# Strassen's seven block products in the last feed-forward stage of a float32 network, with grouped score products and one slot pool

## The chip, the cores and the metric

The kernel runs on one core of one Trainium2 chip, as one program. The metric is the device time of one execution in microseconds (us); lower is better. TensorE (PE) multiplies out of SBUF into PSUM, with its weight loads shown as a row of their own (PEld). VectorE (DVE), ScalarE (ACT) and GpSimd (POOL) do the elementwise work, and SyncE (SP) issues the loads of the weights.

## The reference

Two networks run one after the other on 512 tokens of width 1024, all in float32: two layers with retention, linear recurrence, dilated attention, memory cross-attention and a convolutional feed-forward block, then two layers whose normalised inputs are modulated by a conditioning vector. The last of all stages, ahead of the final norm, is the gated feed-forward block of the second of these layers:

```python
def modulate(h, shift, scale):
    return h * (1.0 + scale) + shift

def swiglu(h, w_gate, w_up, w_down):
    return (jax.nn.silu(h @ w_gate) * (h @ w_up)) @ w_down
```

Here h is 512 x 1024, w_gate and w_up are 1024 x 2816, w_down is 2816 x 1024, and the result is scaled by a gate per channel and added to x. In the layer's first half, a gated linear attention in two directions over four heads is computed; its scores are products of queries and keys that carry the decays.

## The kernel before, in words

Activations lie with channels on partitions: a tile is 128 channels x 512 tokens, so x is eight tiles. Every large product is split in three: an operand becomes a rounded part h and a remainder lo, both in the format that the page calls fp32r, and h*h, h*lo and lo*h are summed in PSUM. So a unit of weights (128 output channels by 1024 inputs) takes 8 x 3 matmuls of 512 columns each.

`raw` (L284) loads a unit by an SP DMA into one of 4 slots (`wr`). `unit` rounds it on ACT (L293, into `wh`, 3 slots) and takes the remainder on DVE (L294, into `wl`, 3 slots). `dx` (L1158) and `dxs` (L1169) issue the matmuls. A scheduler sets each engine's order from the order in the source and the data flow; each engine then runs its own list strictly in order, and semaphores make it wait for others.

`swiglu` is called twice; the second call (l = 1) has no context tokens (`c` is None). It modulates x into eight pairs of tiles (`modulate`, L1102 to L1110), the first 256 tokens ahead of the last 256. The first three weight units run on the first 256 tokens while the others are still being modulated (`dxs`, 144 matmuls of 256 columns). Then `gate_up` takes two units per hidden tile: Silu of the gate on ACT (L1515), the product with the up part on DVE (L1520), and `split` into h (L401, ACT) and lo (L402, DVE). The 22 hidden tiles come in three parts of 8, 8 and 6 (`PARTS`). After each part `gated` multiplies them by w_down, 8 output tiles, and adds into x (L1428). In the last part three of the eight output tiles are done by halves of the tokens, so that the statistics of the final norm start early.

In `cd_mixer`, the attention ahead of it, `head` computes for each of 4 heads and 2 directions four 128 x 128 blocks of scores in one PSUM bank. Each block sums a product over 128 rows (`ZK`, `ZQ`, L1786) and one over 64 rows (`Z2`, L1787), block after block, and a masked copy (L1788) takes the result. The projection of the mixer's output is done like the last part above: its last three output tiles finish in halves of the tokens, and the second halves (the jobs in `r["jobs"]`) are issued by `swiglu`, with steps of the modulation in between.

Tiles of 128 x 512 come from a pool of 66 slots; x tiles have a pool of 9, context tiles (256 wide) one of 9.

## Time and profile before

| what | us |
|---|---|
| median of 3 runs (lowest, highest) | 3156.91 (3155.29, 3159.71) |
| the profiled execution, own time | 3161.09 |
| its span, from first to last instruction | 3159.3 |
| PE busy in the span | 3102.5 (98%) |
| DVE, ACT, POOL busy in the span | 1779.6, 1118.1, 436.7 |

The profile is of one execution. Busy matmuls overlap each other, so PE's pace is read from how many start in a stretch, not from the duration of one. "x" ahead of a number counts instructions, "<-" ahead of an engine names what ended an idle stretch, and the granted clock is 1.00 at 2.4 GHz and 0.50 at 1.2 GHz.

### The profile page before, as it was taken

The numbers are of one execution on the slowest core, as the hardware profiler recorded it, in microseconds if no ns is written. First come the engines' busy times: TensorE is split into PE (matmuls) and PEld (weight loads), VectorE is DVE, ScalarE is ACT, GpSimd is POOL, SyncE is SP. The second block draws the span as 40 slices with busy tenths as digits, with TensorE's granted clock in tenths as the row PEclk, the third lists the DMA queues.
The fourth block names the chain that finished last, engine by engine and source line by source line (L and its number), as shares of the span: only waits on it lengthen the run. The fifth ranks groups of instructions, "written<-read, shape, count | busy, mean of one in ns | idle before, by whom it ended". The sixth has DMA issues, their size and how long they took to land. (4 is left out here: it accounts for less than half of the span.)

```text
span 3159.3 us, 40998 instructions
## 1 busy us (share of the span) xinstructions
PE 3102.5 (98%) x16292; PEld 2590.3 (82%) x16292; DVE 1779.6 (56%) x2894; ACT 1118.1 (35%) x1859; POOL 436.7 (14%) x375
## 2 busy tenths in 40 slices
PE   8999999999999999999999999999999999999998
PEld 6878888888877888888878778888888877788887
DVE  7767676575658857768654467342322453543333
ACT  2225353232445544423343545211212452342222
POOL 5023111010112111101121112000000310120001
PEclk9999999999999999999999999999999999999999
DMA  4224323333323423334342013232211220132222
GB/s 170 78 76 155 115 84 117 117 120 122 128 94 112 144 77 113 121 124 162 129 146 93 23 40 119 96 105 85 78 67 51 89 80 31 36 102 95 99 96 72
DMA packets 110355, 312.80 MB, mean 99 GB/s; under 512 B 12178, under 2 KB 17683, under 8 KB 110163
## 3 DMA queue, kind: packets, MB, share of 16 engines
q1 hardware_dynamic: 101968, 297.32, 27.7%
q10 hardware_dynamic: 8194, 12.86, 1.3%
q8 instruction: 128, 2.10, 0.3%
q14 instruction: 65, 0.52, 0.1%
HBM read 306.98 MB, written 3.15 MB: 98 GB/s over the span
## 5 line engine op out<-in xcount | busy, mean ns | idle before, releaser
L1158 PE MATMUL m<-t,wh 128*128 128x512 f32 (+1 forms) x4124 | 1093.0, 353 | 1.1 <-DVE t L1110 0.4
L293 ACT CAST wh<-wr 128x1024 fp32r<-128x1024 f32 (+2 forms) x485 | 487.8, 1008 | 1244.2 <-PE m L1158 422.2
L294 DVE TENSOR_TENSOR wl<-wr,wh 128x1024 fp32r<-128x1024 f32 (+2 forms) x485 | 579.2, 1195 | 450.1 <-ACT wh L293 438.3
L1158 PEld LDWEIGHTS m<-t,wh 128*128 128x128 f32 x4124 | 726.3, 190 | 115.3 <-issue 11.6
L312 PE MATMUL m<-t,wh 128*128 128x512 f32 (+1 forms) x2576 | 772.9, 383 | 0.0
L1158 PE MATMUL m<-t,wl 128*128 128x512 f32 (+1 forms) x2062 | 724.8, 352 | 0.5 <-DVE wl L294 0.5
L312 PEld LDWEIGHTS m<-t,wh 128*128 128x128 f32 x2576 | 474.1, 188 | 89.8 <-issue 1.0
L312 PE MATMUL m<-t,wl 128*128 128x512 f32 (+1 forms) x1288 | 491.5, 382 | 0.0
L1158 PEld LDWEIGHTS m<-t,wl 128*128 128x128 f32 x2062 | 390.8, 190 | 52.7 <-issue 1.9
L312 PEld LDWEIGHTS m<-t,wl 128*128 128x128 f32 x1288 | 242.7, 188 | 46.2 <-issue 0.7
L428 POOL TENSOR_TENSOR t<-t,t 128x512 f32<-128x512 f32 (+1 forms) x90 | 115.8, 1293 | 1162.8 <-ACT t L423 1162.4
L1062 DVE SCALAR_TENSOR_TENSOR t<-t,silc,t 128x512 f32<-128x512 f32 x280 | 219.0, 810 | 16.5 <-DMA t<-w_ada 15.8
L939 PE MATMUL m<-t,wh 128*128 128x512 f32 x704 | 217.3, 390 | 0.0
L342 PE MATMUL m<-t,wh 128*128 128x512 f32 x496 | 160.1, 402 | 7.3 <-ACT wh L293 7.3
L939 PEld LDWEIGHTS m<-t,wh 128*128 128x128 f32 x704 | 131.9, 188 | 27.2
L906 POOL TENSOR_TENSOR t<-t,t 128x512 f32<-128x512 f32 x44 | 64.5, 1465 | 549.8 <-ACT t L905 540.2
L401 ACT CAST t<-t 128x512 fp32r<-128x512 f32 x116 | 72.0, 621 | 189.0 <-DVE t L1520 104.0
L939 PE MATMUL m<-t,wl 128*128 128x512 f32 x352 | 137.1, 389 | 0.0
L1428 DVE SCALAR_TENSOR_TENSOR x<-m,modt,x 128x512 f32<-128x512 f32 (+1 forms) x70 | 49.3, 705 | 154.2 <-PE m L1158 154.1
L411 POOL TENSOR_TENSOR s<-s,nh 128x4 f32<-128x4 f32 (+2 forms) x67 | 72.1, 1078 | 439.3 <-DVE s L471 161.3
L357 PE MATMUL m<-wh,t 128*128 128x512 f32 x384 | 123.2, 397 | 0.0
L342 PEld LDWEIGHTS m<-t,wh 128*128 128x128 f32 x496 | 93.6, 192 | 26.7 <-ACT wh L293 8.0
(387 smaller groups left out, 3405.7 us busy)
## 6 DMA issues: line engine op xcount, KB each, us to landing
t<-w_ada SPq DMA_DIRECT2D x192, 256.0 KB, 4.0
wr<-w_fi SPq DMA_DIRECT2D x88, 512.0 KB, 3.3
wr<-w_gu SPq DMA_DIRECT2D x88, 512.0 KB, 3.3
wr<-w_fo SPq DMA_DIRECT2D x32, 512.0 KB, 3.4
wr<-w_dn SPq DMA_DIRECT2D x32, 512.0 KB, 3.2
wr<-w_ev SPq DMA_DIRECT2D x24, 512.0 KB, 3.3
wr<-w_xk SPq DMA_DIRECT2D x16, 512.0 KB, 3.4
wr<-w_xv SPq DMA_DIRECT2D x16, 512.0 KB, 3.4
```

What stands on the lines that cost most here:

```text
L293: nc.scalar.copy(h[:, 0:e], r[:, 0:e])
L294: nc.vector.tensor_sub(lo[:, 0:e], r[:, 0:e], h[:, 0:e])
L312: nc.tensor.matmul(ps[:, 0:n], A[:, s], B[:, 0:n], start=c == 0, stop=c == tot - 1)
L342: self.nc.tensor.matmul(ps, A[:, s], B, start=k == 0 and i == 0, stop=k == K - 1 and i == 2)
L357: nc.tensor.matmul(pss[tb], A[:, ts], B[:, s], start=(u == 0 and j == 0 and i == 0), stop=(u == nu - 1 and j == kper - 1 and i == 2))
L401: nc.scalar.copy(h[:, 0:n], src[:, 0:n])
L411: self.nc.gpsimd.tensor_tensor(r, v, self.nh[:, 0:w], ALU.pow)
L428: e.tensor_tensor(st[0][:, 0:n], st[0][:, 0:n], sq[:, 0:n], ALU.add)
L906: nc.gpsimd.tensor_tensor(y, y, rb, ALU.mult)
L939: nc.tensor.matmul(ps[:, 0:n], A[:, s], B[:, 0:n], start=c == 0, stop=c == tot - 1)
L1062: nc.vector.scalar_tensor_tensor(acc[i], r, s, acc[i], ALU.mult, ALU.add)
L1158: nc.tensor.matmul(ps[:, s], A[:, ws], B[:, s], start=j == 0 and i == 0, stop=j == last and i == 2)
```

## The change

**The last feed-forward stage.** For l = 1 a new function `swiglu_w` replaces the loops. It takes two units of weights as one 2 x 2 block matrix and the activations as another (two groups of input tiles by two halves of the tokens), and forms the 2 x 2 result with seven block products (Strassen's scheme in Winograd's form) where before there were eight. A pair is a gate unit with its up unit, or two output tiles of w_down over three inputs each side.

- `w_pair` loads both units (r0 and r1). Four sums of halves of them, s0, s1, s3 and s2, are made on POOL in this order (`start`, L1580 to L1583 of the new file; width 512 for a gate pair, 384 for a w_down pair). Each of the seven products (m1, m5, m6, m3, m2, m7, m4 in order of issue) rounds its own weight block by `operand` (ACT L325, DVE L326), which is 512 or 384 columns wide, and then runs 12 (w_down: 9) matmuls of 256 columns (L1594).
- Bank A sums m1, m6, m7 and m4 one after the other, bank C sums m5 and m3. Partial values are taken out in between: on ACT after m1, m5 and m6, on DVE after m3 (L1613), m2 (L1618) and m7 (L1622); for these the next product into the bank has to wait. m4 of a pair is issued after m1 and m5 of the next pair (`w_push`).
- The activations need seven variants too. `w_first` makes those for m1 and m2, `w_combos` the other five, with two subtractions on DVE and two on POOL, casts and remainders. This is done once for the four pairs of input tiles, and for 9 pairs of the first 18 hidden tiles. The last 4 hidden tiles go through `gated` as before.
- There are 22 gate pairs and 12 w_down pairs (three rounds of four), in the order 7 gate, 4 down, 6 gate, 4 down, 6 gate, 4 down, 3 gate, and then `gated` on the rest.
- `modulate_f` writes the modulated x in float32 for this, in place of `modulate`.

**Grouped score products.** In `head`, the eight 64-row products of both directions are issued first, then the eight 128-row products, in two banks.

**Pools.** x and context tiles (two to a slot) come from the one pool, now 78 slots. Raw units have 3 slots instead of 4. Rounded operands are tiles of 512 columns with h and lo side by side, 8 slots (four units); so `unit` now issues two casts and two subtractions for a unit of 1024 columns everywhere in the kernel.

```diff
-NSLOT = 66
+NSLOT = 78
...
+def fm_units_eo(w):
+    k, m = w.shape
+    t = np.concatenate([w, np.zeros((24 * 128 - k, m), w.dtype)], axis=0).reshape(4, 6, 128, m)
+    t = np.concatenate([t[:3, [0, 2, 4, 1, 3, 5]], t[3:]], axis=0)
+    return fm_units(t.reshape(24 * 128, m), 6)
...
-        self.xp = E(tc.tile_pool(name="xp", bufs=9))
-        self.cx = E(tc.tile_pool(name="cx", bufs=9))
         self.A = E(tc.tile_pool(name="A", bufs=NSLOT))
...
-        self.wr = E(tc.tile_pool(name="wr", bufs=4))
-        self.wh = E(tc.tile_pool(name="wh", bufs=3))
-        self.wl = E(tc.tile_pool(name="wl", bufs=3))
+        self.wr = E(tc.tile_pool(name="wr", bufs=3))
+        self.wk = E(tc.tile_pool(name="wk", bufs=8))
...
+    def operand(self, src):
+        nc, n = self.nc, src.shape[-1]
+        k = self.wk.tile([128, 1024], F32R, tag="k", name=f"wk{self.n}")
+        nc.scalar.copy(k[:, 0:n], src)
+        nc.vector.tensor_sub(k[:, 512:512 + n], src, k[:, 0:n])
+        return k
     def unit(self, ap):
...
-        nc.scalar.copy(h[:, 0:e], r[:, 0:e])
-        nc.vector.tensor_sub(lo[:, 0:e], r[:, 0:e], h[:, 0:e])
-        return h, lo
+        ks = [self.operand(r[:, c:min(c + 512, e)]) for c in range(0, e, 512)]
+        return Part(ks, 0), Part(ks, 512)
...
+    def w_combos(self, t0, t1, first=None):
+        P, Q = slice(0, 256), slice(256, 512)
+        out = first or self.w_first(t0, t1)
+        u, v = self.T(), self.T()
+        nc.vector.tensor_sub(u[:, P], t0[:, Q], t0[:, P])
+        nc.gpsimd.tensor_tensor(u[:, Q], t1[:, Q], t0[:, Q], ALU.subtract)
+        nc.vector.tensor_sub(v[:, P], t1[:, Q], u[:, P])
+        nc.gpsimd.tensor_tensor(v[:, Q], t1[:, P], v[:, P], ALU.subtract)
+        h, lo = self.T(F32R), self.T(F32R)
+        nc.scalar.copy(h[:, P], t1[:, Q])
+        nc.vector.tensor_sub(lo[:, P], t1[:, Q], h[:, P])
+        out["m3"] = (h[:, P], lo[:, P])
+        h, lo = self.split(u)
+        out["m5"], out["m7"] = (h[:, P], lo[:, P]), (h[:, Q], lo[:, Q])
+        h, lo = self.split(v)
+        out["m6"], out["m4"] = (h[:, P], lo[:, P]), (h[:, Q], lo[:, Q])
+        return out
+    def w_first(self, t0, t1):
+        for name, t in (("m1", t0), ("m2", t1)):
+            k = self.T(F32R)
+            nc.scalar.copy(k[:, 0:256], t[:, 0:256])
+            nc.vector.tensor_sub(k[:, 256:512], t[:, 0:256], k[:, 0:256])
+            out[name] = (k[:, 0:256], k[:, 256:512])
...
+    def w_pair(self, a0, a1, xs, done):
+        hw = 128 * len(xs)
+        def start():
+            r0, r1 = self.raw(a0), self.raw(a1)
+            s = [self.T() for _ in range(4)]
+            add = nc.gpsimd.tensor_tensor
+            L, R = slice(0, hw), slice(hw, 2 * hw)
+            add(s[0][:, L], r1[:, L], r1[:, R], ALU.add)
+            add(s[1][:, L], s[0][:, L], r0[:, L], ALU.subtract)
+            add(s[3][:, L], r0[:, R], s[1][:, L], ALU.subtract)
+            add(s[2][:, L], r0[:, L], r1[:, L], ALU.subtract)
+            st["w"] = {"m1": r0[:, L], "m2": r0[:, R], "m4": r1[:, R], "m5": s[0][:, L], "m6": s[1][:, L], "m3": s[3][:, L], "m7": s[2][:, L]}
+            st["A"], st["mu"] = self.PM(), self.T()
+        def mul(name, bank, first, last):
+            w = self.operand(st["w"][name])
+            ps, n = st[bank], len(xs)
+            for k in range(n):
+                s, t = slice(k * 128, k * 128 + 128), slice(512 + k * 128, 640 + k * 128)
+                xh, xl = xs[k][name]
+                for i, (A, B) in enumerate(((w[:, s], xh), (w[:, s], xl), (w[:, t], xh))):
+                    nc.tensor.matmul(ps[:, 0:256], A, B, start=first and k == 0 and i == 0, stop=k == n - 1 and i == 2, skip_group_check=not first)
+        def m1():
+            start()
+            mul("m1", "A", True, False)
+            nc.scalar.copy(st["mu"][:, 0:256], st["A"][:, 0:256])
...
+        def m7():
+            mul("m7", "A", False, False)
+            nc.vector.tensor_add(st["m5"][:, 256:512], st["A"][:, 0:256], st["m5"][:, 0:256])
+        def m4():
+            mul("m4", "A", False, True)
+            done(st["top"], st["A"][:, 0:256], st["m5"][:, 256:512])
+        return list(zip((0, 1, 3, 4, 5, 6, 9), (m1, m5, m6, m3, m2, m7, m4)))
...
+    def swiglu_w(self, l, r):
...
+        late = self.modulate_f(x, r["sx2"], l, 3, ts, 256, H[1])
+        next(late)
+        next(late)
+        xs = [self.w_first(ts[k], ts[k + 4]) for k in range(4)]
+        self.run(late)
+        for k in range(4):
+            self.w_combos(ts[k], ts[k + 4], xs[k])
...
+        def gate_up(j):
+            def done(gate, up0, up1):
+                nc.scalar.activation(gate, gate, AF.Silu)
+                y = self.T()
+                nc.vector.tensor_mul(y[:, 0:256], up0, gate[:, 0:256])
+                nc.vector.tensor_mul(y[:, 256:512], up1, gate[:, 256:512])
+                if j >= 18:
+                    tail.append(self.split(y))
+                    return
+                ys.append(y)
+                if len(ys) == 2:
+                    hid.append(self.w_combos(*ys))
+                    ys.clear()
+            self.w_push((wi[j], wi[22 + j], xs, done))
+        def down(p, m, hs):
+            def done(top, b0, b1):
+                nc.vector.scalar_tensor_tensor(x[m], top, self.M(l, 5, 0, m), x[m], ALU.mult, ALU.add)
+                for s, b in zip(H, (b0, b1)):
+                    nc.vector.scalar_tensor_tensor(x[m + 1][:, s], b, self.M(l, 5, 0, m + 1), x[m + 1][:, s], ALU.mult, ALU.add)
+            self.w_push((wd[m * 4 + p], wd[m * 4 + 4 + p], hs, done))
...
+        return self.gated(f"w_dn{l}", lambda m: 4 * m + 3, tail, [], x, None, l, 5, halves=3)
     def swiglu(self, l, r):
         nc = self.nc
         x, c = r["x"], r["c"]
+        if not c:
+            return self.swiglu_w(l, r)
...
-            for d, SC in ((0, SCf), (1, SCb)):
-                ZQ, ZK = Z[d]
-                ps = self.PA()
+            pss = [self.PA(), self.PA()]
+            for d in range(2):
                 for j in range(4):
                     s = slice(j * 128, j * 128 + 128)
-                    nc.tensor.matmul(ps[:, s], ZK[:, s], ZQ[:, s], start=True, stop=False)
-                    nc.tensor.matmul(ps[:, s], Z2[d][1][P, s], Z2[d][0][P, s], start=False, stop=True)
+                    nc.tensor.matmul(pss[d][:, s], Z2[d][1][P, s], Z2[d][0][P, s], start=j == 0, stop=False)
+            for d in range(2):
+                ZQ, ZK = Z[d]
+                for j in range(4):
+                    s = slice(j * 128, j * 128 + 128)
+                    nc.tensor.matmul(pss[d][:, s], ZK[:, s], ZQ[:, s], start=False, stop=j == 3)
```

How the scheduler's order stands, at three places. Line numbers of the changed program are those of the new file.

DVE in the last stage, before: in one round of `gate_up` (tile names: wl and wh parts of weights, wr raw weights, m a PSUM bank, t tiles).

```order
L294 TENSOR_TENSOR wl3786_24903<-wr3786_24900,wh3786_24902 128x1024
L402 TENSOR_TENSOR t3778_24828<-t3774_24793,t3777_24827 128x512
L294 TENSOR_TENSOR wl3789_24936<-wr3789_24933,wh3789_24935 128x1024
L1520 TENSOR_TENSOR t3781_24862<-m3783_24870,t3781_24862 128x512
L294 TENSOR_TENSOR wl3793_24972<-wr3793_24969,wh3793_24971 128x1024
```

DVE in the last stage now, one gate pair (raw units wr4969 and wr4970) and what is left of the pair ahead of it (wr4950). In order: the operand of m1, L1613 of the pair ahead, m5, L1618 of the pair ahead, m4 of the pair ahead, m6, L1622 of the pair ahead, then m3, m2 and m7.

```order
L326 TENSOR_TENSOR wk4977_26142<-wr4969_26128,wk4977_26142 128x512
L1613 TENSOR_TENSOR t4965_26093<-m4958_26025,t4956_26008 128x256
L326 TENSOR_TENSOR wk4980_26160<-t4971_26132,wk4980_26160 128x512
L1618 TENSOR_TENSOR t4965_26093<-a4966_26095,t4956_26008 128x256
L326 TENSOR_TENSOR wk4981_26176<-wr4950_25997,wk4981_26176 128x512
L326 TENSOR_TENSOR wk4993_26219<-t4972_26133,wk4993_26219 128x512
L1622 TENSOR_TENSOR t4959_26026<-m4955_26007,t4959_26026 128x256
L326 TENSOR_TENSOR wk4994_26235<-t4974_26135,wk4994_26235 128x512
L326 TENSOR_TENSOR wk4997_26253<-wr4969_26128,wk4997_26253 128x512
L326 TENSOR_TENSOR wk4998_26269<-t4973_26134,wk4998_26269 128x512
```

Where two subtractions of 1024 columns stood for 48 matmuls of 512 columns, seven of 512 columns now stand for 84 matmuls of 256, with evictions between them. On ACT the casts stand in the same order, and the Silu of the pair ahead (L1673) stands between the casts of m4 and m6:

```order
L325 CAST wk4980_26160<-t4971_26132 128x512
L325 CAST wk4981_26176<-wr4950_25997 128x512
L325 CAST wk4993_26219<-t4972_26133 128x512
L325 CAST wk4994_26235<-t4974_26135 128x512
L1673 ACTIVATE t4965_26093<-t4965_26093 128x512
```

In this pair it stands behind the casts of m6 and m3, in the pair ahead of it between those of m4 and m6; both orders occur.

SP in the same place, the loads of three pairs with the engines that each waits for. There are three slots, so the second load of a pair goes into the slot of the first unit of the pair ahead. That is free when m2's operand of that pair has been taken on DVE and its s2 made on POOL.

```order
L317 DMA wr4949_25995<-w_gu1 128x1024 [waits DMAHW3_49,DVE_49]
L317 DMA wr4950_25997<-w_gu1 128x1024 [waits DMAHW4_49,DVE_49,Pool_49]
L317 DMA wr4969_26128<-w_gu1 128x1024 [waits DMAHW5_49,DVE_49]
L317 DMA wr4970_26130<-w_gu1 128x1024 [waits DMAHW6_49,DVE_49,Pool_49]
L317 DMA wr4999_26285<-w_gu1 128x1024 [waits DMAHW7_49,DVE_49]
```

Before, a load waited only for the remainder (L294) of the unit four ahead of it, and POOL had nothing to do here. POOL now, for a pair and the start of the next, with the two subtractions of `w_combos` (L1529, L1531) between them:

```order
L1580 TENSOR_TENSOR t4971_26132<-wr4970_26130 128x512
L1581 TENSOR_TENSOR t4972_26133<-t4971_26132,wr4969_26128 128x512
L1582 TENSOR_TENSOR t4974_26135<-wr4969_26128,t4972_26133 128x512
L1583 TENSOR_TENSOR t4973_26134<-wr4969_26128,wr4970_26130 128x512
L1529 TENSOR_TENSOR t4985_26201<-t4982_26192,t4962_26059 128x256
L1531 TENSOR_TENSOR t4986_26202<-t4982_26192,t4986_26202 128x256
L1580 TENSOR_TENSOR t5001_26289<-wr5000_26287 128x512
```

POOL's first sum of a pair reads the second raw unit, and L1529 ahead of the next pair's first sum reads the hidden tile (t4982) of the pair ahead.

PE in `head` before, and now:

```order
L1786 MATMUL a3433_22430<-t3272_21367,t3273_21368 128x128
L1787 MATMUL a3433_22430<-t3276_21371,t3277_21372 128x128
L1786 MATMUL a3433_22430<-t3272_21367,t3273_21368 128x128
L1787 MATMUL a3433_22430<-t3276_21371,t3277_21372 128x128
L1786 MATMUL a3433_22430<-t3272_21367,t3273_21368 128x128
```

```order
L2014 MATMUL a4377_23145<-t4176_22046,t4177_22047 128x128 x4
L2014 MATMUL a4378_23146<-t4178_22048,t4179_22049 128x128 x4
L2019 MATMUL a4377_23145<-t4172_22042,t4173_22043 128x128 x4
L2019 MATMUL a4378_23146<-t4174_22044,t4175_22045 128x128 x4
```

The 64-row and the 128-row products alternated 16 times per head, and now stand in two runs of eight (L2014 and L2019).

## Rows read from the trace of the kernel before

**Rows 1.** The page, busy time of each engine over the span.
```profile
PE 3102.5 (98%) x16292; PEld 2590.3 (82%) x16292; DVE 1779.6 (56%) x2894; ACT 1118.1 (35%) x1859; POOL 436.7 (14%) x375
```
**Rows 2.** Busy time by stretch: last stage in full run, and the heads.
```profile
2804.50:3119.00 314.50, 314.48 (x1387) 260.56 (x1388) 112.17 (x120) 85.06 (x105) 0.00 (x0) 1.00 0.29 98
...
2640.00:2742.00 102.00, 101.68 (x588) 77.04 (x587) 46.37 (x101) 28.89 (x54) 9.23 (x12) 1.00 0.04 11
```
**Rows 3.** Instructions of L1169 and L1158 in the last stage: ns min/median/max, starts.
```profile
L1169 PE MATMUL m<-t,wh x96: 278/284/562, 2784.2 to 2802.6; 128*128 128x256 f32 x96
...
L1158 PE MATMUL m<-t,wl x522: 279/390/501, 2804.5 to 3148.2; 128*128 128x512 f32 x162, 128*128 128x256 f32 x12
```
**Rows 4.** Timeline of PE, half-width matmuls of the last output tiles (start, us, count).
```profile
3144.12 0.40 PE L1158 MATMUL m<-t,wh 128*128 128x256 f32 x2
...
3145.20 0.40 PE L1158 MATMUL m<-t,wh 128*128 128x256 f32 x2
```
**Rows 5.** Who waited for whom in the last stage: total us, times, longest.
```profile
PE m L1158 <- DVE wl L294: 0.5, 1, 0.5
```
**Rows 6.** Groups by shape, 2740 to 3160 and whole span: busy us, mean ns.
```profile
L294 DVE TENSOR_TENSOR wl<-wr,wh 128x1024 fp32r<-128x1024 f32 x60 | 73.6, 1227 | 84.0 <-ACT wh L293 79.8
L293 ACT CAST wh<-wr 128x1024 fp32r<-128x1024 f32 x60 | 63.2, 1053 | 224.0 <-PE m L1158 151.4 <-issue 64.0 <-PE m L1169 8.5
L401 ACT CAST t<-t 128x512 fp32r<-128x512 f32 x24 | 14.9, 621 | 3.8 <-POOL t L1813 3.5
L1103 ACT ACTIVATE t<-t,modt 128x256 fp32r<-128x256 f32 x10 | 4.9, 503 | 2.1 <-DVE t L1102 2.1
L1100 ACT CAST t<-t 128x256 fp32r<-128x256 f32 x6 | 2.4, 398 | 0.1
...
L1428 DVE SCALAR_TENSOR_TENSOR x<-m,modt,x 128x512 f32<-128x512 f32 x26 | 19.5, 751 | 70.8 <-PE m L1158 70.8
L1428 DVE SCALAR_TENSOR_TENSOR x<-m,modt,x 128x256 f32<-128x256 f32 x12 | 5.8, 483 | 9.2 <-PE m L1158 9.2
...
L1523 DVE TENSOR_TENSOR t<-m,t 128x256 f32<-128x256 f32 x22 | 9.3, 425 | 16.9 <-PE m L1158 16.9
L1376 POOL TENSOR_TENSOR t<-t,nam 128x256 f32<-128x256 f32 x24 | 16.9, 738 | 105.5 <-DMA t<-nab 70.3 <-PE m L1158 35.1
```
**Rows 7.** DMA issues of weights: KB each, median us to landing.
```profile
wr<-w_gu SPq DMA_DIRECT2D x88, 512.0 KB, 3.3
...
wr<-w_dn SPq DMA_DIRECT2D x16, 384.0 KB, 2.8
```
**Rows 8.** Timeline of DVE and of POOL, each with the other idle.
```profile
2811.90 0.68 DVE L402 TENSOR_TENSOR t<-t,t 128x512 fp32r<-128x512 f32 x1
...
1928.79 1.29 POOL L428 TENSOR_TENSOR t<-t,t 128x512 f32<-128x512 f32 x1 [1.74 <-ACT t L423]
```
**Rows 9.** Timeline of DVE and POOL in the same stretches, both at work.
```profile
12.26 9.50 DVE L405 SCALAR_TENSOR_TENSOR t<-xin,vec,t 128x512 fp32r<-128x512 f32 x6
...
13.31 1.61 POOL L515 TENSOR_TENSOR t<-t,t 128x512 f32<-128x512 f32 x1
14.88 1.49 POOL L513 TENSOR_TENSOR t<-xin 128x512 f32<-128x512 f32 x1
...
1912.52 1.33 DVE L294 TENSOR_TENSOR wl<-wr,wh 128x512 fp32r<-128x512 f32 x1
```
**Rows 10.** Timeline of PE in a head: start, us, count.
```profile
2645.14 0.61 PE L1774 MATMUL a<-t,t 64*128 64x128 f32 x4
2645.59 1.03 PE L1776 MATMUL a<-t 64*128 64x256 f32 x4
2646.54 0.49 PE L1786 MATMUL a<-t,t 128*128 128x128 f32 x2
...
2647.38 0.49 PE L1786 MATMUL a<-t,t 128*128 128x128 f32 x2
```
**Rows 11.** Opening of the last stage: busy time by stretch, and PE's timeline.
```profile
2778.00:2782.00 4.00, 0.60 (x3) 0.39 (x4) 3.37 (x5) 1.67 (x3) 3.40 (x3) 0.78 0.86 262
2782.00:2786.00 4.00, 2.96 (x14) 2.88 (x15) 2.40 (x8) 3.02 (x7) 2.51 (x3) 0.50 0.34 125
...
2785.20 0.42 PE L1169 MATMUL m<-t,wl 128*128 128x256 f32 x1
2785.41 0.42 PE L1169 MATMUL m<-t,wh 128*128 128x256 f32 x1
```

More of the change, by code (lines that the diff above doesn't have):

```diff
@@ L223, in layout, with __init__, __getitem__ @@
     return a
+class Part:
+    def __init__(self, tiles, base):
+        self.tiles, self.base = tiles, base
+    def __getitem__(self, key):
+        c = key[1]
+        o = self.base + c.start % 512
+        return self.tiles[c.start // 512][key[0], o:o + c.stop - c.start]
 class Net:
@@ L242, in __init__ @@
         self.side = None
+        self.half = None
         self.early = []
@@ L248, in T, with X, C @@
         return self.A.tile([128, 512], dt, tag="t", name=f"t{self.n}")
+    def X(self):
+        self.n += 1
+        return self.A.tile([128, 512], F32, tag="t", name=f"x{self.n}")
+    def C(self):
+        if self.half is None:
+            self.n += 1
+            t = self.A.tile([128, 512], F32, tag="t", name=f"c{self.n}")
+            self.half = t[:, 256:512]
+            return t[:, 0:256]
+        t, self.half = self.half, None
+        return t
     def S(self, w=16):
@@ L1446, in gated @@
             wt = self.wt(w, u(m), len(yx))
-            t = self.xp.tile([128, 512], F32, tag="x", name=f"x{self.n}") if m < 8 - halves else x[m]
+            t = self.X() if m < 8 - halves else x[m]
             r["x"].append(t)
@@ new lines, in w_first, with w_push @@
+    def w_first(self, t0, t1):
+        nc = self.nc
+        out = {}
+        for name, t in (("m1", t0), ("m2", t1)):
[3 more added lines that the diff above has]
+            out[name] = (k[:, 0:256], k[:, 256:512])
+        return out
+    def w_push(self, pair=None):
+        q = self.queue
+        if pair is not None:
+            ev = self.w_pair(*pair)
+            t = 7 * self.pushed
+            self.pushed += 1
+            q += [(t + at, self.pushed, f) for at, f in ev]
+            q.sort(key=lambda e: e[:2])
+            until = t + 7
+        else:
+            until = None
+        while q and (until is None or q[0][0] < until):
+            q.pop(0)[2]()
@@ new lines, in w_pair, with m5, m6, m3 @@
+    def w_pair(self, a0, a1, xs, done):
+        nc = self.nc
+        self.tick()
+        hw = 128 * len(xs)
+        st = {}
+        def start():
[21 more added lines that the diff above has]
+            nc.scalar.copy(st["mu"][:, 0:256], st["A"][:, 0:256])
+        def m5():
+            st["C"], st["m5"] = self.PM(), self.T()
+            mul("m5", "C", True, False)
+            nc.scalar.copy(st["m5"][:, 0:256], st["C"][:, 0:256])
+        def m6():
+            mul("m6", "A", False, False)
+            nc.scalar.copy(st["mu"][:, 256:512], st["A"][:, 0:256])
+        def m3():
+            mul("m3", "C", False, True)
+            st["top"] = self.T()
+            nc.vector.tensor_add(st["top"][:, 256:512], st["C"][:, 0:256], st["mu"][:, 256:512])
+        def m2():
+            st["B"] = self.PA()
+            mul("m2", "B", True, True)
+            nc.vector.tensor_add(st["top"][:, 0:256], st["B"][:, 0:256], st["mu"][:, 0:256])
+        def m7():
[5 more added lines that the diff above has]
+        return list(zip((0, 1, 3, 4, 5, 6, 9), (m1, m5, m6, m3, m2, m7, m4)))
@@ new lines, in modulate_f @@
+    def modulate_f(self, x, st, l, j, out, n, s):
+        nc = self.nc
+        rstd, _ = self.stat_end(st, n)
+        yield
+        pb = self.bcast(rstd, n)
+        rb = self.T()
+        nc.scalar.copy(rb[:, 0:n], pb[:, 0:n])
+        yield
+        for k in (0, 4, 1, 5, 2, 6, 3, 7):
+            t, sc, sh = out[k][:, s], self.M(l, j + 1, 0, k), self.M(l, j, 0, k)
+            if k in (5, 2, 7):
+                nc.gpsimd.tensor_tensor(t, x[k][:, s], rb[:, 0:n], ALU.mult)
+                nc.scalar.activation(t, t, AF.Identity, bias=sh, scale=sc)
+            else:
+                nc.vector.scalar_tensor_tensor(t, x[k][:, s], sc, pb[:, 0:n], ALU.mult, ALU.mult)
+                nc.scalar.activation(t, t, AF.Identity, bias=sh)
@@ new lines, in swiglu_w @@
+    def swiglu_w(self, l, r):
+        nc, a = self.nc, self.a
+        x = r["x"]
+        H = (slice(0, 256), slice(256, 512))
+        ts = [self.T() for _ in range(8)]
+        mx = self.modulate_f(x, r["sx"], l, 3, ts, 256, H[0])
+        for i, job in enumerate(r["jobs"]):
+            job()
+            if i in (1, 2):
+                next(mx, None)
+        self.run(mx)
+        late = self.modulate_f(x, r["sx2"], l, 3, ts, 256, H[1])
[5 more added lines that the diff above has]
+            self.w_combos(ts[k], ts[k + 4], xs[k])
+        self.queue, self.pushed = [], 0
+        ys, hid, tail = [], [], []
+        wi, wd = a[f"w_gu{l}"], a[f"w_dn{l}"]
+        def gate_up(j):
[18 more added lines that the diff above has]
+            self.w_push((wd[m * 4 + p], wd[m * 4 + 4 + p], hs, done))
+        j = 0
+        for p in range(3):
+            while j < 6 * p + 7:
+                gate_up(j)
+                j += 1
+            hs = hid[0:3]
+            del hid[0:3]
+            for m in (0, 2, 4, 6):
+                down(p, m, hs)
+        while j < 22:
+            gate_up(j)
+            j += 1
+        self.w_push()
+        return self.gated(f"w_dn{l}", lambda m: 4 * m + 3, tail, [], x, None, l, 5, halves=3)
@@ L1565, in small @@
         def small():
-            return self.cx.tile([128, 256], F32, tag="c", name=f"c{self.n}")
+            return self.C()
         def rope(ps, scale, eng=nc.gpsimd):
```

29 lines of the change are left out of this document (15 added, 14 removed).

## The prediction

> **What bounds the kernel now.** I read the page's first line, then the windows, then who waited for whom, then durations by shape. The page gives PE 98% of the span, the others far less [rows 1]. The windows show the same where the change works: in the last stage's full run PE is busy all of the time and starts 1387 matmuls in 314.5 us, .227 us each, with DVE at 36%, ACT at 27% and POOL at nothing; in the heads PE is busy 101.68 of 102 us [rows 2]. So PE's own issue bounds both places. PE waited .5 us in all for a remainder from DVE [rows 5]. The stage begins at 2784.2 and its last matmul starts at 3148.2, so with that matmul's own .1 it takes 364.1 us [rows 3].
>
> **Fewer matmuls.** 256-column matmuls start every .120 us (3145.20 less 3144.12 over nine) [rows 4]. The new stage has 22 gate pairs of 84 and 12 w_down pairs of 63, together 2604: 312.5 us. `gated` on the last four hidden tiles adds 60 of 512 columns (13.6) and 72 of 256 (8.6): 22.3. If PE stayed the bound, the stage would take 334.8, a gain of 29.3. Per pair PE needs 10.1 (gate) or 7.6 (w_down).
>
> **The new chain.** A load takes the slot of the first unit of the pair ahead, and may not start before m2's operand of that pair is on DVE and its s2 on POOL. From that release to the next, in a gate pair: the load lands after 3.3 us [rows 7]; s0, which reads that unit, takes 1.29 on POOL alone [rows 8]; the cast for m5 .62 [rows 6]; then DVE, strictly in order, does the subtractions for m5, m4, m6, m3 and m2, five of .68 alone [rows 8], and two evictions from PSUM of 256 columns at .42 [rows 6]. That is 3.3 + 1.29 + .62 + 3.4 + .84 = 9.5, and some .2 for handovers: 9.7, just under PE's 10.1. Nothing hides an addition here: while this chain is late, PE has only m4 of the pair ahead to do.
>
> While DVE does these five, POOL does s1, s3 and s2. Such meetings cost time: with both at work, six DVE operations on SBUF operands took 9.50 (1.58 each), POOL's took 1.61 and 1.49, and a DVE subtraction of exactly this kind 1.33 against .68 alone [rows 9]. So one DVE and one POOL operation take about 1.58 together, and a meeting costs DVE .65 to .9. I count two of the three in full (s1 partly runs while DVE still waits for m5's cast): +1.8, **11.6 per gate pair** with the handovers. Ends: 10.1 without any meeting (PE is then the bound again), 12.5 with all three.
>
> In pairs with `w_combos` (nine), DVE has between m2's subtraction and the next m5's: m7 and the next m1 (1.36), two products (.85), five operations of 256 columns (2.1), two of 512 (1.36) and two evictions (.85), 6.5 us, where load, sum and cast give it 5.2: +1.3. The second product waits for m4 of that pair on PE (.6), and one more meeting falls there, as POOL's L1529 and L1531 (.74 each [rows 6]) stand ahead of s0 and push it back: **14.2**; without meetings 12.0. I worked the 34 pairs through with each engine's order; these are its means.
>
> A w_down pair: load 2.8 [rows 7], and between the 512- and 256-column rows about 1.0 on POOL, .5 on ACT and .55 on DVE for 384 columns: 2.8 + 1.0 + .5 + 2.75 + .84 evictions and 1.23 for the adds into x (.75 and .48 [rows 6]) = 9.1; two meetings of .6 make 10.3, one of four rounds' pairs has fewer and is near 9: mean **10.0**, without meetings 9.25.
>
> Pairs: 13 x 11.6 + 9 x 14.2 + 12 x 10.0 = 398.6.
>
> The Trainium skill, "SBUF — State Buffer", section "Who interferes with whom", says that a DVE instruction with two SBUF inputs contends with a GpSimd instruction that reads SBUF, and calls the shared ports an exclusive lock. Rows 9 agree that they meet, but there each pays part: 1.58 for both, not the 1.97 of one behind the other. By its lock for a whole instruction two meetings would cost 2 x 1.29 = 2.6 a pair instead of 1.8, 27 us more in all.
>
> **The opening.** Before, 144 half-width matmuls [rows 3] run while the second half of the tokens is modulated. Now only m1 (1.4 us) can run; m5 needs `w_combos` of both halves, for all four pairs of tiles. On ACT that is 16 modulations at .50, 8 casts at .40 for `w_first`, 4 x (.40 + 2 x .62) for `w_combos`, and three operands at .62 [rows 6]: 8.0 + 3.2 + 6.6 + 1.9 = 19.7, begun near 2782 (ACT busy 3.02 of the 4 us from there [rows 11]); DVE has as much. So m5 can't run through before some 2804, where PE could have gone on from 2785.6: 18 us, of which the first two pairs give back about 4, as their weights are ready and they run at PE's pace. I take **14**, between 8 (the split before was also paced by these engines) and 18.
>
> Stage: 398.6 + 14 + 22.3 = 434.9, against 364.1: **+70.8**.
>
> **Grouped scores.** In a head now, two alternating blocks take .84 (2646.54 to 2647.38), so eight 6.7; four 64-row matmuls that follow each other start within .45 (2645.14 to 2645.59), .112 each [rows 10]. Grouped, 32 matmuls at .112 are 3.6 and two changes of shape .3: 3.9. That gains 2.7 a head in a place where PE is the bound, **−10.9** for four; ends 0 (the wait for the banks moves to DVE's masked copies) and −12.
>
> **The rest.** The first operand at the kernel's start is 512 wide: a cast of .62 for 1.05 and a subtraction of .68 for 1.23, **−1.0**, once. Elsewhere two casts of 512 cost ACT .19 more per unit and DVE .13 [rows 6]; both lie beside PE's work, 24 matmuls or 5.4 us per unit, with DVE at 56% [rows 1]. Were that cover gone, each unit would cost up to .19; PE's .5 us of waiting [rows 5] speaks against it. Slots: three raw and four rounded units are as deep as four and three, and the 78 common slots hold what 84 or less held in three pools: nothing.
>
> Sum: 70.8 − 10.9 − 1.0 = +58.9 on the profiled execution's 3161.1: 3220.0. That execution lies 4.2 above the median of the runs, so I predict **3216**.
>
> **Rivals.**
> 1. The other side, faster: the chain through the three slots stays shorter than PE's time in nearly every pair. It has .4 us of room in a plain gate pair without meetings [rows 8], has none with one meeting, and the loads may land sooner when two follow each other. Then 334.8 + 14 − 364.1 − 11.9 = −27, 3130. It decides at a mean pair: gain and loss balance at (364.1 + 11.9 − 36.3) / 34 = 10.0 us, where PE needs 9.2 and I forecast 11.7. Rows 9 speak against it. Chance .13.
> 2. The meetings are hidden: 13 x 10.1 + 9 x 12.0 + 12 x 9.25 = 350.3 instead of 398.6, so +10.6, 3167. For it: subtractions from POOL's pause (load) are untouched. Near it lies no change (a mean pair of 10.0). Chance .18.
> 3. Every meeting counts, or each lasts a whole instruction: +.9 x 34 = +31, 3246; both, 3 x 1.29 a pair, +70, 3286. Chance .12. The lock of the Trainium skill's page on SBUF is this case; rows 9 bear it out only in part, so it gets no more.
> 4. The clock: ahead of the stage PE is busy only .60 of 4 us, and the granted clock falls from .78 there to .50 (1.2 GHz) in the next 4, with 256-column matmuls .21 apart [rows 11]. The forecast leaves PE idle some 2.5 us a pair. If one pair in four runs at that level (gate 84 x .21 = 17.6), 8 x 6 = +48: 3265. PE's idle time is in pieces of 1 to 2 us, between busy stretches. Chance .05.
> 5. That the stage's products aren't fewer can be left out: the program's order has them.
>
> **Numbers.** Forecast case .52, rivals .13, .18, .12, .05. The range of 3165 to 3262 leaves out rival 1, rival 4 and the far end of rival 3, some .2. A measurement tells .2% (6.3 us) from no change: faster .14 (rival 1 and a little of 2), same .03 (the crossing between rivals 1 and 2), slower .83.
>
> **What would show it.** In the profile after: some 2.4 us of PE idle per pair, with the operands' subtractions (L326) as what ended it; loads of w_gu1 that start right after m2's subtraction or s2; subtractions of 512 columns in the stage at a mean near 1.0, against .68, and POOL's sums above 1.29; PE idle near 2786 to 2804; heads about 2.7 us shorter each; the same matmul pace of .12. It is wrong if PE is busy over 97% of the stage (rival 1), if the subtractions stay at .68 (rival 2), or if the granted clock in the stage falls under .9 (rival 4).

## The result and the profile after

| | before | changed |
|---|---|---|
| median of the runs, us (4 runs each) | 3158.31 | 3251.30 |
| lowest and highest, us | 3155.29, 3164.78 | 3249.94, 3252.32 |
| span of the profiled execution, us | 3159.3 | 3249.5 |

The changed kernel takes 1.0288 times as long (95% interval 1.0276 to 1.0300), 93 us more. I had forecast 59 more (3216), with a range of 3165 to 3262; the time lies in it and on the side I gave .83.

The page's first line, which answers to [rows 1]: DVE has 269 us more to do and POOL 185 more, while PE's busy time is the same, as waits have taken the place of matmuls.

```profile
PE 3103.6 (96%) x17318; PEld 2632.8 (81%) x17318; DVE 2049.1 (63%) x3658; ACT 1295.8 (40%) x2565; POOL 621.4 (19%) x537
```

The last stage by stretch, for [rows 2, 11] (busy time of PE, PEld, DVE, ACT, POOL, then granted clock, DMA share, GB/s): the opening, the 34 pairs with their end, and `gated` on the rest.

```profile
2793.00:2813.40 20.40, 3.72 (x12) 2.84 (x12) 19.26 (x34) 12.35 (x28) 11.52 (x13) 0.50 0.00 0
2813.40:3217.00 403.60, 349.14 (x2602) 330.11 (x2602) 323.70 (x493) 197.42 (x418) 203.62 (x153) 0.96 0.26 83
3217.00:3238.00 21.00, 20.67 (x125) 18.28 (x126) 7.81 (x14) 7.23 (x20) 8.56 (x12) 1.00 0.01 2
```

The stage begins at 2793.0, and its last matmuls start near 3238.5, so it takes 445.5 us where it took 364.1: +81.4 (forecast +70.8). In the opening PE did 12 matmuls in 20.4 us.

One turn of the chain, from the chain of waits between 2880 and 2915 (start, us, what). This is the order that the prediction gave: load, s0, cast, then subtractions on DVE with evictions among them.

```profile
2881.17 4.02 DMA wr<-w_gu
...
2885.33 1.29 POOL t L1580
2886.65 0.63 ACT wk L325
...
2888.47 0.41 DVE t L1618
2888.88 1.53 DVE wk L326 x2
...
2891.84 0.41 DVE t L1622
2892.25 1.24 DVE wk L326 x3
```

s0 (L1580) is made once per pair. Its row by line (ns min/median/max, first and last start) gives the pairs' pace: 3196.3 less 2811.0 over 33 pairs is 11.68 us.

```profile
L1580 POOL TENSOR_TENSOR t<-wr x34: 1010/1288/1741, 2811.0 to 3196.3; 128x512 f32<-128x512 f32 x22, 128x384 f32<-128x384 f32 x12
```

Groups by shape between 2820 and 3215 (busy us, mean ns | idle before, and what ended it):

```profile
L326 DVE TENSOR_TENSOR wk<-t,wk 128x512 fp32r<-128x512 f32 x84 | 81.9, 985 | 34.6 <-ACT wk L325 34.6
L326 DVE TENSOR_TENSOR wk<-wr,wk 128x512 fp32r<-128x512 f32 x71 | 67.9, 956 | 6.0 <-ACT wk L325 5.9
...
L1583 POOL TENSOR_TENSOR t<-wr,wr 128x512 f32<-128x512 f32 x21 | 35.9, 1707 | 0.0
L1582 POOL TENSOR_TENSOR t<-wr,t 128x512 f32<-128x512 f32 x21 | 34.0, 1619 | 1.6
...
L1580 POOL TENSOR_TENSOR t<-wr 128x512 f32<-128x512 f32 x21 | 29.1, 1385 | 87.6 <-DMA wr<-w_gu 76.4 <-DVE t L1618 5.8 <-DVE x L1688 5.3
```

A subtraction of 512 columns takes .97 on average where it takes .68 alone [rows 8], and POOL's sums 1.39 to 1.71 where 1.29. POOL's first sum of the gate pairs waits 76.4 us for loads: the load stands in the chain.

The heads, PE's timeline, for [rows 10]: two runs of 16, and 2666.47 to 2670.33 is 3.86 us, where eight alternating block pairs took 6.7.

```profile
2666.47 1.95 PE L2014 MATMUL a<-t,t 64*128 64x128 f32 x16
2668.34 2.05 PE L2019 MATMUL a<-t,t 128*128 128x128 f32 x16
2670.33 0.71 PE L2003 MATMUL a<-t,t 64*128 64x128 f32 x4
```

But the program is 20.0 us late when the heads begin (L2003 first starts at 2663.75; before, L1774 at 2643.73), where I had expected to be 1 us ahead.

### The profile page after: what moved, and what is told of

Read it like the earlier page. It is cut to its first block, busy times and chain, and to the rows that moved or that the text cites. A ratio compares the mean times of both kernels' runs of the same rounds, so it can differ in the third digit from the quotient of the medians.

```text
span 3249.5 us, 45317 instructions
## 1 busy us (share of the span) xinstructions
PE 3103.6 (96%) x17318; PEld 2632.8 (81%) x17318; DVE 2049.1 (63%) x3658; ACT 1295.8 (40%) x2565; POOL 621.4 (19%) x537
## 4 chain that ended last, share of the span: by engine, by line
PE 68%; DVE 9%; issue 4%; DMA 4%; ACT 3%; POOL 3%; SPq 0%; ACTq 0%; POOLq 0%; DVEq 0%
PE m L1196 25%; PE m L350 19%; PE m L977 6%; PE m L380 4%; DVE wk L326 4%; PE m L395 3%; DMA wr<-w_gu 1%; PE m L1240 1%; DMA t<-w_ada 1%; DMA wr<-w_dn 1%; ACT wk L325 1%; POOL t L1580 1%; PE m L1207 1%; PE a L433 1%; PE m L1594 1%
## 5 line engine op out<-in xcount | busy, mean ns | idle before, releaser
L326 DVE TENSOR_TENSOR wk<-wr,wk 128x512 fp32r<-128x512 f32 (+2 forms) x912 | 673.9, 745 | 431.5 <-ACT wk L325 428.9
L325 ACT CAST wk<-wr 128x512 fp32r<-128x512 f32 (+2 forms) x912 | 552.5, 609 | 921.9 <-PE m L350 259.7
L1196 PE MATMUL m<-t,wk 128*128 128x512 f32 (+1 forms) x4752 | 872.5, 343 | 4.9 <-ACT t L439 1.3
L350 PE MATMUL m<-t,wk 128*128 128x512 f32 (+1 forms) x3864 | 859.5, 381 | 0.0
L1196 PEld LDWEIGHTS m<-t,wk 128*128 128x128 f32 x4752 | 742.2, 191 | 118.0 <-issue 12.9
L350 PEld LDWEIGHTS m<-t,wk 128*128 128x128 f32 x3864 | 696.8, 188 | 135.8 <-issue 1.7
L1594 PE MATMUL m<-t,wk 128*128 128x256 f32 x2232 | 311.5, 296 | 71.5 <-ACT wk L325 22.7
L1594 PEld LDWEIGHTS m<-t,wk 128*128 128x128 f32 x2232 | 289.1, 200 | 90.9 <-ACT wk L325 38.7
L977 PE MATMUL m<-t,wk 128*128 128x512 f32 x1056 | 242.0, 390 | 1.1 <-ACT t L439 0.8
L977 PEld LDWEIGHTS m<-t,wk 128*128 128x128 f32 x1056 | 197.8, 188 | 42.7 <-ACT t L439 1.3
L380 PE MATMUL m<-t,wk 128*128 128x512 f32 x744 | 180.9, 396 | 16.9 <-ACT t L442 10.8
L380 PEld LDWEIGHTS m<-t,wk 128*128 128x128 f32 x744 | 138.3, 190 | 46.3 <-ACT t L442 10.8
L439 ACT CAST t<-t 128x512 fp32r<-128x512 f32 x124 | 76.5, 621 | 223.4 <-DVE t L1749 111.7
L326 DVE TENSOR_TENSOR wk<-t,wk 128x512 fp32r<-128x512 f32 (+1 forms) x136 | 116.8, 873 | 49.7 <-ACT wk L325 49.3
L395 PE MATMUL m<-wk,t 128*128 128x512 f32 x576 | 139.2, 397 | 0.0
L440 DVE TENSOR_TENSOR t<-t,t 128x512 fp32r<-128x512 f32 x124 | 104.0, 842 | 49.3 <-ACT t L439 44.3
L325 ACT CAST wk<-t 128x512 fp32r<-128x512 f32 (+1 forms) x136 | 78.5, 580 | 124.4 <-POOL t L1580 86.0
L395 PEld LDWEIGHTS m<-wk,t 128*128 128x128 f32 x576 | 107.4, 190 | 21.3
```

What stands on the lines that cost most here:

```text
L325: nc.scalar.copy(k[:, 0:n], src)
L326: nc.vector.tensor_sub(k[:, 512:512 + n], src, k[:, 0:n])
L350: nc.tensor.matmul(ps[:, 0:n], A[:, s], B[:, 0:n], start=c == 0, stop=c == tot - 1)
L380: self.nc.tensor.matmul(ps, A[:, s], B, start=k == 0 and i == 0, stop=k == K - 1 and i == 2)
L395: nc.tensor.matmul(pss[tb], A[:, ts], B[:, s], start=(u == 0 and j == 0 and i == 0), stop=(u == nu - 1 and j == kper - 1 and i == 2))
L439: nc.scalar.copy(h[:, 0:n], src[:, 0:n])
```

## The experiments

Each median was taken beside runs of the kernel before on the same chip, but not all experiments ran on one chip. So where a few us matter, the ratio to the kernel before is given, with its 95% interval.

**Grouped scores alone.** The kernel before with the new loops in `head`.

> The kernel before with the grouped score products alone. My theory (the alternation of 64-row and 128-row products cost PE .42 us per two of them and PE bounds the heads): 10.9 us less, about 3147, and 3.9 us per head from its first 64-row product to its last 128-row one, against 6.7. Rival: the gain is lost in waits for the two banks or for the masked copies that now come later; then within 3 us of 3158. Second rival: the 11 us between the heads and the last stage's begin in the changed kernel came from the pools; then again no change here.

3147.22, ratio .9965 (.9952 to .9979). The 11 us are there without any other part of the change. This kernel is faster than both, and only the one with the common pool (below) is level with it.

**Everything but the last stage.** The changed kernel without `swiglu_w`:

```diff
-        if not c:
-            return self.swiglu_w(l, r)
```

> The changed kernel with the old loops in the last stage (and the old layout of w_down there); grouped scores and the pools stay. In the changed kernel the program stands 20 us behind the one before when the heads begin, where I had 1 us of gain. Theory: the pools and the halved operands cost these 20 us, whatever the last stage does: 3158 + 20 - 11 = 3167. Rival: the scheduler moved work because of the new last stage, and the pools cost nothing: 3158 - 11 = 3147.

3164.13, ratio 1.0011 (1.0002 to 1.0020): the first theory. Pools and halved operands cost 17 us against grouped scores alone by the medians, 15 by the ratios, and the new last stage 87 (3251.3 − 3164.1).

**Four raw slots with the old last stage.**

```diff
-        self.wr = E(tc.tile_pool(name="wr", bufs=3))
-        self.wk = E(tc.tile_pool(name="wk", bufs=8))
+        self.wr = E(tc.tile_pool(name="wr", bufs=4))
+        self.wk = E(tc.tile_pool(name="wk", bufs=7))
```

> As the kernel without Strassen's products, with 4 raw slots as before in place of 3, paid for by one operand slot (7 for 8). If the third raw slot less is what costs the 20 us (loads that start later), most of it comes back: 3147 to 3152. If halved operands (more instructions on ACT and DVE) or the common pool cost it, it stays at 3165 to 3170.

3162.73, with the same ratio, 1.0011. The missing raw slot, in exchange for one operand slot more, is not what costs the 17 us there.

**Halved operands alone, the common pool alone, and both.** Each on top of grouped scores, in the kernel before: `operand` and `Part` with six slots; `X` and `C` with `NSLOT = 79`; and both.

> The kernel before with grouped scores and operands of 512 columns (two casts and two subtractions per unit, six slots, three units deep as before); raw slots, x and context pools as before. With grouped scores alone the time was 3147, with all pools of the change 3164, and a fourth raw slot gave nothing back. Theory: halved operands cost the 16 us: 3160 to 3166. Rival: the common slot pool does: 3145 to 3150. A part of both lies between.

3156.44, ratio .9985 (.9976 to .9994): 9 us of the 17 by the medians, 6 of the 15 by the ratios, less than the theory asked.

> The kernel before with grouped scores and x and context tiles in the common pool (79 slots, the same memory in all); operands and raw slots as before. Theory (the halved operands cost the 16 us): 3145 to 3150. Rival (the common pool, whose slots come free in another order, does): 3160 to 3166.

3148.36, ratio .9955 (.9941 to .9969): the common pool costs nothing that can be measured.

> The kernel before with grouped scores, operands of 512 columns (six slots) and the common pool (79 slots), 4 raw slots. Alone, the operands took the 3147 of grouped scores to 3156 and the pool to 3148; all of the change but the last stage stands at 3164. Theory (the two costs add up, and what is left comes from the counts of slots, 78, 8 and 3): 3156 to 3159. Rival (together they cost more than apart): 3162 to 3166.

3157.92, ratio .9993 (.9984 to 1.0002), where the theory had it: 9 us by the ratios, which fits a sum of the two. The intervals leave each of these differences open by some 4 to 5 us, so the sum is not shown closely. The 5 to 6 us between this and 3163 or 3164 go with the numbers of slots (79 and 6 here, 78 and 7 or 8 there). Which of them, and how, stays open.

The profiles show where the time goes, though not why. If the kernel without `swiglu_w` and grouped scores alone are laid beside each other matmul by matmul, the first is 5.9 us behind at 1766 us and 18.4 at 2009. In that stretch PE's products of queries and keys (L1364, L1326 before) wait for the exponentials of a softmax on ACT (L1271, L1233 before). First grouped scores alone, then without `swiglu_w` (us, times, longest):

```profile
PE a L1326 <- ACT t L1233: 3.6, 4, 1.3
...
PE a L1364 <- ACT t L1271: 7.5, 5, 2.6
```

In the same stretch halved operands alone lose 6.3 us, and the common pool alone 7.8, which it had gained earlier.

**Four raw slots in the changed kernel**, the edit shown above.

> The changed kernel with 4 raw slots for 3 (and 7 operand slots for 8). A pair's second load then waits for m4's operand of two pairs before, and no longer for m2's and s2 of the pair ahead. Theory (load, sum, cast and five subtractions follow each other through the slot): the 3.4 us of the load leave the chain; the next bound is DVE, busy 82% from 2800 to 3140, so the 34 pairs fall from 403 us to 330 to 350, the whole to 3180 to 3200. Rival (DVE with its meetings is the bound already, and the slot only shows where it waits): under 15 us less, 3236 or more.

3182.95: 68 us less than the changed kernel, inside the theory's span. The pace falls to (3129.2 − 2804.2) / 33 = 9.85 us. Windows from 2830 to 3130, first of this kernel:

```profile
2830.00:3130.00 300.00, 285.41 (x2303) 278.28 (x2302) 296.23 (x442) 170.21 (x367) 189.25 (x139) 1.00 0.29 97
```

DVE is now busy 296 of 300 us: it is the bound, and no longer the load.

**One sum in place of four.** s1, s3 and s2 are left out, and m6, m3 and m7 read s0.

```diff
-            s = [self.T() for _ in range(4)]
+            s = [self.T()] * 4
...
-            add(s[1][:, L], s[0][:, L], r0[:, L], ALU.subtract)
-            add(s[3][:, L], r0[:, R], s[1][:, L], ALU.subtract)
-            add(s[2][:, L], r0[:, L], r1[:, L], ALU.subtract)
```

> The changed kernel with s0 alone made on POOL; s1, s3 and s2 are left out and m6, m3 and m7 take s0 in their place, so these products are not those of the reference. Theory (subtractions on DVE that meet POOL's sums take .98 us for .68, and that lies on the chain): plain gate pairs fall from 11.7 to 10.1 (PE), pairs with combinations from 14 to 12, w_down pairs from 10.3 to 9.3: some 50 us less, 3200. Rival (the meetings fall beside waits for the load): under 15 us less.

3191.94: 59 us less. In its groups by shape the subtractions, unchanged in number and size, are back at the duration that they have alone (window 2820 to 3130):

```profile
L326 DVE TENSOR_TENSOR wk<-t,wk 128x512 fp32r<-128x512 f32 x76 | 51.0, 682 | 28.2 <-ACT wk L325 28.2
L326 DVE TENSOR_TENSOR wk<-wr,wk 128x512 fp32r<-128x512 f32 x57 | 39.0, 684 | 16.3 <-ACT wk L325 16.3
```

This also takes away the time in which ACT's casts wait for s1, s3 and s2, so not all of the 59 is the meetings. The next run keeps the sums.

**The four sums on DVE.**

```diff
-            add = nc.gpsimd.tensor_tensor
+            add = nc.vector.tensor_tensor
```

> The changed kernel with the four sums of a pair on DVE in place of POOL. DVE gets 4 x .68 = 2.7 us more of work per gate pair, and no sum of a pair meets it. Theory (each meeting costs DVE .65 to .9, and s0 on DVE is .6 shorter): chain of 3.3 + .68 + .62 + 3.4 + .84 + 2.0 = 10.9 per plain gate pair for 11.7, so 15 to 30 us less, 3220 to 3236. Rival (meetings cost little, DVE's work counts): 2.0 to 2.7 us more per pair, 3300 or more.

3210.12: 41 us less, more than the theory gave, though DVE issues 136 operations more. It isn't the meetings alone, as s0 on DVE is also .6 shorter and stands in the chain. The pace is (3158.2 − 2811.2) / 33 = 10.52. Subtractions and sums all take their own time now:

```profile
L326 DVE TENSOR_TENSOR wk<-t,wk 128x512 fp32r<-128x512 f32 x72 | 49.4, 699 | 0.1
...
L1581 DVE TENSOR_TENSOR t<-t,wr 128x512 f32<-128x512 f32 x18 | 12.4, 690 | 0.5
```

Work of .68 per sum on the busier engine is cheaper than the same work beside it.

**Four raw slots, and the sums on DVE.** Both edits.

> The changed kernel with 4 raw slots and the four sums of a pair on DVE. With 4 slots alone DVE was busy 98% of the stage. Theory (then DVE's occupancy is the bound, and a sum on DVE costs it .68 where a sum on POOL costs it up to .9, but not every one on POOL meets a DVE operation): about the time of 4 slots alone, 3175 to 3205, with plain gate pairs at PE's 10.1 and pairs with combinations at 12 to 13. Rival (only meetings hold DVE): 3165 or less.

3173.34: 10 us less than four slots alone, just below the theory's span and above the rival's. So in this stage a sum on POOL costs more, on average, than the .68 that it takes on DVE. The pace is (3121.8 − 2804.0) / 33 = 9.63, near PE's own 9.2. Windows of this kernel, its opening and its pairs:

```profile
2784.60:2805.30 20.70, 3.72 (x12) 2.84 (x12) 19.64 (x35) 12.36 (x29) 9.28 (x11) 0.50 0.00 0
2830.00:3130.00 300.00, 295.60 (x2369) 287.00 (x2368) 289.61 (x578) 173.12 (x378) 21.82 (x18) 1.00 0.31 99
```

PE is busy 295.6 of 300 us, nearly as before the change. Still the kernel (ratio 1.0038) is 9 to 11 us slower than the one with the same slots and the old last stage (3162.73, ratio 1.0011): the opening of 20.7 us eats most of what the fewer products save.

**Two pairs ahead in the opening.** The first two gate pairs stand ahead of the second half's modulation, all seven products on the operands of m1 and m2; so the first two hidden tiles differ from the reference's.

```diff
-            self.w_push((wi[j], wi[22 + j], xs, done))
+            self.w_push((wi[j], wi[22 + j], first if j < 2 else xs, done))
...
+        gate_up(0)
+        gate_up(1)
+        self.run(late)
+        for k in range(4):
+            self.w_combos(ts[k], ts[k + 4], xs[k])
```

> The changed kernel with the first two gate pairs issued ahead of the modulation of the second 256 tokens, all seven products on the operands of m1 and m2; so the first two hidden tiles are not those of the reference, all work stays. Theory (PE idles 18 to 20 us in the opening because m5 waits for the combinations of all eight tiles, and two pairs are 20 us of PE's work): 10 to 18 us less, 3233 to 3241. Rival (ACT and DVE are full with modulation and combinations there, and the pairs' own operands stand in their queues): under 5 us less.

3245.88: 5.4 us less, nearly the rival's case (ratio 1.0267 against 1.0288). PE's timeline shows the wait moved behind the two pairs:

```profile
2817.96 3.04 PE L1594 MATMUL m<-t,wk 128*128 128x256 f32 x24
2831.83 1.10 PE L1594 MATMUL m<-t,wk 128*128 128x256 f32 x3 [10.83 <-ACT wk L325]
```

The work for the combinations has to be done all the same, and the two pairs' operands stood in its way on DVE. The edit also brought POOL's sums of the first pair forward, beside DVE's eight remainders of `w_first` (L1549): these took 8.36 us in a row where they took 4.07. So the place of the matmuls is not what holds the opening. That DVE does is argued from its 19.26 busy us of 20.4; no run takes work off it there.

## Why the prediction was right, and where it was too small

The time is 35 us above the 3216 that I gave. In the profiles, 10.6 of these lie in the last stage. Another 20.7 lie ahead of it: it begins 8.8 us later than before, where I had it 11.9 earlier. The last 4.2 are what I took off because the execution profiled before lay above its median; the changed kernel's does not.

**The chain and its pace: right in the mean, with luck.** I forecast 398.6 us for 34 pairs, 11.72 each; measured 11.68. The chain of waits shows load, s0, cast and subtractions in this order. But the parts were off and cancelled. From one s0 to the next, the twelve gate turns without `w_combos` took 12.4 us on average (forecast 11.6), the nine with it 12.5 (14.2), and the w_down turns 10.3 (10.0). The first is near the 12.5 that I had given for three meetings, where I counted two. The 2.6 us that I added for `w_combos` hardly show, as the load then lands beside DVE's work for it:

```profile
2949.85 1.28 POOL L1580 TENSOR_TENSOR t<-wr 128x512 f32<-128x512 f32 x1 [5.68 <-DMA wr<-w_gu]
...
2961.83 0.79 POOL L1531 TENSOR_TENSOR t<-t,t 128x256 f32<-128x256 f32 x1 [2.37 <-DVE t L1530]
2962.58 1.74 POOL L1580 TENSOR_TENSOR t<-wr 128x512 f32<-128x512 f32 x1
...
2974.82 1.29 POOL L1580 TENSOR_TENSOR t<-wr 128x512 f32<-128x512 f32 x1 [5.42 <-DMA wr<-w_gu]
```

The turn with `w_combos` (from 2949.85) takes 12.73, and its successor's s0 waits for no load; the turn without (from 2962.58) takes 12.24, and the next s0 waits 5.42 for its load.

Four slots gave 68 us, the sums on DVE 41, and both together 78, so the gains overlap. Four slots alone left 25 of the 93 us, the sums on DVE alone 52. Only with both was PE nearly the bound again.

**The meetings: right in size, wrong in kind.** The mean of .97 less .68, over seven subtractions, is 2.0 us per gate pair, where I counted 1.8 on the path. But I had read [rows 9] as each engine paying a part of a meeting, and that reading failed. Here is a turn on both engines, first POOL, then DVE:

```profile
2951.21 1.30 POOL L1581 TENSOR_TENSOR t<-t,wr 128x512 f32<-128x512 f32 x1
2952.59 1.62 POOL L1582 TENSOR_TENSOR t<-wr,t 128x512 f32<-128x512 f32 x1
2954.16 1.73 POOL L1583 TENSOR_TENSOR t<-wr,wr 128x512 f32<-128x512 f32 x1
...
2951.82 1.24 DVE L326 TENSOR_TENSOR wk<-t,wk 128x512 fp32r<-128x512 f32 x1 [1.91 <-ACT wk L325]
2952.98 1.77 DVE L326 TENSOR_TENSOR wk<-wr,wk 128x512 fp32r<-128x512 f32 x1
2954.68 0.41 DVE L1622 TENSOR_TENSOR t<-m,t 128x256 f32<-128x256 f32 x1
```

The first subtraction ends at 2953.06, .55 us after POOL's L1581 (2952.51). The second ends at 2954.75, .54 after L1582 (2954.21). The trace has this for every one of the 59 subtractions of 512 columns between 2820 and 3215 that began while POOL was at an operation: each ends .55 after that operation, whether it had .54 or 1.23 us left, and they take 1.44 on average. The 91 that met none took .68, and the four that began ahead of POOL's operation .69. With four raw slots it is the same, 68 of 68.

So the subtraction that comes second waits until POOL's whole operation is over, and a meeting costs what is left of it, .76 on average. POOL waits likewise: its 51 sums of 512 columns that began during such a subtraction (L326 or L440) took 1.66 on average for 1.29, and ended 1.14 after it. That is the exclusive lock that I had quoted from the Trainium skill, "SBUF — State Buffer", section "Who interferes with whom", and the trace agrees with it. My 1.29 per meeting for that case was too much, since the wait is only for what is left. L294 of [rows 9] shows it already. POOL's sum beside it began at 1912.00, so with the 1.29 of [rows 8] it ended near 1913.29, and L294 ended at 1913.85.

Rival 2 (meetings hidden) falls, as its sign, subtractions at .68, did not come and taking the sums away gave 59 us. How much of these 59, or of the 41, is meetings alone was not separated. Rival 1 falls with the pace.

**The opening: too small.** I took 14, from 18 less 4 that the first two pairs would give back. From the stage's begin to the first s0 it is 18.0, m5 went on 20.4 us after m1, and nothing came back: the second s0 stands 11.43 after the first (2811.01 and 2822.44). The step that failed is "the first two pairs give back about 4, as their weights are ready". With three slots the second pair's second load waits for m2's operand of the first pair like any other. With four slots, where it doesn't, the second s0 came 6.7 us after the first (2804.17 and 2810.88). The 18 itself was summed for ACT, which was busy only 12.35 us there; it was DVE, which I had put at "as much", that was. Also, the last part of those 20 us is a relay: for each pair of tiles DVE, POOL, DVE, POOL, ACT and DVE take turns, 3.4 us a round:

```profile
2805.87 0.41 DVE L1528 TENSOR_TENSOR t<-t 128x256 f32<-128x256 f32 x1
2806.31 0.42 DVE L1530 TENSOR_TENSOR t<-t,t 128x256 f32<-128x256 f32 x1
2806.66 0.42 DVE L1534 TENSOR_TENSOR t<-t,t 128x256 fp32r<-128x256 f32 x1
2807.02 2.31 DVE L440 TENSOR_TENSOR t<-t,t 128x512 fp32r<-128x512 f32 x2
2809.26 0.41 DVE L1528 TENSOR_TENSOR t<-t 128x256 f32<-128x256 f32 x1
```

**The end of the pairs: forgotten.** I gave each pair one pace. From the last s0 (3196.3) to the long run of `gated` (3217.3) it is 21.0 us, 9.3 more than a pace. The chain of waits there holds three loads of units of w_down, which come one after the other through the raw slots, and the split of a last hidden tile (L439), which stands on ACT behind the cast that waits for the third load:

```profile
3204.47 2.50 DMA wr<-w_dn
...
3208.42 2.48 DMA wr<-w_dn
...
3212.37 3.66 DMA wr<-w_dn
...
3216.75 0.53 ACT t L439
```

With four slots and the sums on DVE the same stretch is 14.6 us (3121.8 to 3136.4), 5.0 more than its pace. Opening +4 and this +9.3, less 1.6 on the pace and about 1 on `gated`, are the 10.6 by which the stage was under-sized.

**Grouped scores: right.** 10.9 forecast; 3.86 us per head as worked out, and 12 us between the medians of the two kernels, 11 by the ratio.

**"The rest": wrong, and the largest miss.** I put the halved operands and the pools at −1.0 because their work lies beside PE's. They cost 15 to 17 us: 6 to 9 the operands, nothing measurable the pool, 5 to 6 tied to numbers of slots and open. The sentence that failed is that PE's .5 us of waiting [rows 5] speaks against a cost: that row is of the last stage alone, and the operands are made in every stage, also where PE waits for ACT. The profiles put most of the loss between 1766 and 2009 us, where it does. What in the halved operands or the slots lengthens that wait is not shown.

**The clock: right to leave out.** The granted clock was .50 (1.2 GHz) in the opening, where PE ran 12 matmuls in 20.4 us, and .96 from 2813.4 to 3217. So rival 4's price, one pair in four at the low level, did not come, although PE stood idle for 54 of those 404 us.

## What to carry to other kernels

Count the work that a product-saving scheme puts on the other engines per unit of PE time, and follow the buffer that it holds longest: here one raw slot put a load of 3.4 us into each turn, and one slot more was worth 68 us. Price two engines that meet by the starts and ends of single operations and not by means: here one waited for the end of the other's whole operation. Then add what happens at both ends of the pipeline, since an opening that needs all combinations first cost 20 us where the scheme saves 29. A change of helpers that serve the whole program (operand sizes, pools) has to be costed in the stages where PE waits, not only in the stage that one is looking at. And a mean that comes out right is worth splitting, as two wrong parts can make it.
